# One 512 KB transfer for a cache page's keys and values, in one slot held until the value products

## The chip, the cores and the metric

The kernel runs on one core of a Trainium2 chip. The metric is the device time of one execution in microseconds (us). Before the change it was 1029.4 us, the median of 3 runs (1027.76 to 1031.65).

## What is computed

One layer of a decoder step for 544 tokens of 1024 channels: 512 tokens of a new prompt, and 32 sample tokens (8 sequences of 4 tokens), which continue sequences of 4096 past positions. All of it is in 32-bit floating point.

```python
glu_a, glu_b, q, k, v, g_conv, g_att = split(x @ w_in)            # 512,512,512,512,512,1024,1024 columns
conv_out = silu(layer_norm(depthwise_conv31(glu_a * sigmoid(glu_b)))) @ w_conv_proj
att_out  = stick_breaking_attention(q, [past_k, k], [past_v, v]) @ w_att_proj    # 8 heads of 64
x = layer_norm(ALPHA * x + (sigmoid(g_conv) * conv_out + sigmoid(g_att) * att_out) @ w_out)
gate, up = split(x @ w_ffn_up)                                    # 2 * 2816 columns
x = layer_norm(ALPHA * x + (silu(gate) * up) @ w_ffn_down + sigmoid(x @ w_ple_gate) * (p @ w_ple))
# for each query, positions s before it, from the last to the first:
#   weight(s) = exp(log_sigmoid(z_s) + sum over later t of log_sigmoid(-z_t)),  z = q . k / 8 + bias
```

The past keys and values of the 8 sample sequences lie in a pool of 320 pages of 128 positions; `page_table` names the 32 pages of each sequence. A page in the kernel's layout is 128 rows of 4 KB: in each row 2 KB belong to the keys (transposed: 4 pairs of heads by 128 positions) and the next 2 KB to the values of one position. The cache that is read has 8 x 32 pages of 512 KB, 134 MB.

## The kernel before

**One instruction order, made by a planner.** The kernel is written as Python generators ("streams"): the dense products (`main`), the weights' loader and splitter, the convolution, the prompt's attention, the loads of the cache (`prefetch`), the scores over the cache (`scores`), the rest of the cache attention (`decode`), and the sample tokens' way to the first norm (`sample_tail`). A class `Weave` runs them and emits their instructions in one order by estimated times: TensorE's clock `t`, and clocks for ScalarE, VectorE, GpSimd and the DMAs. A stream that yields a number, a time or a condition is resumed when the estimated clock is there; the first stream in order of priority that can go is taken, and the dense products come last. On the chip each engine takes its instructions in that order and waits on semaphores; the planner's times matter only for the order. `moved` adds a transfer to the DMA clock: a start 1.5 us ahead at the earliest, and its bytes divided by 0.357e6 per us; `load` counts the tile as there 1.5 us later.

**Dense products.** A weight unit is 128 x 1024 (512 KB), loaded on SyncE's queue (SP) and split in two parts, so that each product is three products (`g<-xh,wh` and the like in the profile). The sequence is: 20 column tiles for q, k, conv and v; 8 tiles for the attention gate (flags `("ga", c)`); 8 for the convolution's gate (flags `("gc", c)`); the attention's projection (its end sets the flag `"ga"`); the convolution's projection; `w_out` in two passes over halves of the prompt; the feed-forward's first 4 column tiles with the first 256 tokens, then the same with all others. This last pass needs the sample tokens' first norm, so it waits for the whole cache attention and `sample_tail`. After it come the rest of the feed-forward and the second norm.

**The cache attention.** It has 32 steps ("chunks"): 4 sequences by 2 pages each, 16 chunks from the last position to the first, and then the other 4 sequences. Of one chunk:

- `prefetch` loads in SP's queue: first the keys, then the values; a slot of 512 KB takes the keys (or values) of both pages of one sequence, by two transfers of 256 KB. The page's number is read into a register ahead of each keys' transfer (L536) and used again for the values. So there are 4 slots of keys and 4 of values for each chunk.
- `scores` (L552): 16 products of 32 queries with 256 positions into bank `z`, four sequences side by side in TensorE's columns (the trace shows each as two matmuls). Then its 4 slots are free: `cur["kv"] -= 4`. ScalarE follows with four operations on `zb` and `l`.
- `decode` (L605): VectorE's running sum over positions, which carries on from the chunk before, an exponential, two transposes, a copy, and then the value products `av`, 8 products with 512 columns (16 matmuls in the trace). Then the 4 slots of values are free.

**Room.** `slot` takes one of 39 slots of 512 KB, which dense tiles use too. `room_kv` lets `prefetch` go on only while the cache holds fewer slots than allowed at this place of the order:

```python
KVMAX = 17
KVROOM = (("ga", 17), (("gc", 0), 13), (("ga", 4), 15))
```

so 17 until the fifth gate tile of the attention, then 15, from the first gate tile of the convolution 13, and from the end of the attention's projection 17 again. `sample_tail` takes its 12 weight units under the same limit once all of the cache is loaded. `KMARGIN` = 1.0 us stands between a chunk's last key and its scores.

Of the kernel before, what the change touches and what calls it, by code (L numbers as in the profile page):

```python
# [20 lines left out]
NT = 544          # 512 prompt tokens, then 32 sample tokens  # L21
HT = 272
HA = 256          # the first half of the tokens in the passes that take them by halves
KW = 31
NPG = 32
POOL = 320
NA = 4            # column tiles of the feed-forward that start with half of the tokens
EMB = (1, 2)
FA = []           # their units of weights, and those of w_ple between them
# [8 lines left out]
# where a unit lies: the passes over the second half of the tokens take weights again  # L38
# [4 lines left out]
# columns of the vector table  # L43
# [6 lines left out]
class At:  # L50
    """A time to wait for."""
# [5 lines left out]
class Weave:  # L57
    """Emits the steps of several streams in one program order, by estimated times of the engines."""
# [9 lines left out]
    def op(self, clock, us, out, reads):  # L68
        """An instruction's estimated time: returns its end."""
        start = max([getattr(self, clock), self.t] + [self.ready.get(a.name, 0.0) for a in reads])  # L70
        setattr(self, clock, start + us)
        self.ready[out.name] = max(self.ready.get(out.name, 0.0), start + us + LAT)

    def take(self, tag, tile, bufs=1):
        """A new owner of a bank: it may be written when the one before has been read."""
# [5 lines left out]
    def bank(self, tag):  # L81
        """True when the bank's owner has been read."""
        return lambda: not self.owner.get(tag) or self.read.get(self.owner[tag][0], 1e9) <= self.t
# [44 lines left out]
class Engine:  # L128
    """An engine's instructions, with their estimated times."""
# [39 lines left out]
def step_kernel(ctx: ExitStack, tc: tile.TileContext, xT, pT, kv, state, pt, W, cv, cc, yT, kT, vT, cvo):  # L169
# [15 lines left out]
    def spare(n):  # L185
        """Waits until n of the short-lived tiles can be had."""
# [12 lines left out]
    def room():  # L199
        """Waits until the bank pair that comes next will have been read."""  # L200
# [13 lines left out]
    def moved(ap):  # L214
# [3 lines left out]
        wv.dma = max(wv.dma, wv.t + 1.5) + n / 0.357e6  # L218
# [36 lines left out]
    def tt(out, in0, in1, op):  # L255
        """An operation of two tensors in SBUF, on the vector engine or on GpSimd."""
# [27 lines left out]
    def sigmoid(out, in_, t, t2, then, more=None):  # L284
        """out = exp(-(max(-x, 0) + log(1 + exp(-|x|)))); t2 views t in the form of in_."""
# [42 lines left out]
    def held(u):  # L328
        """Where a unit's parts stay while both halves of the tokens need them."""
# [13 lines left out]
    def w_split(u, e):  # L343
        """Half a unit's parts."""
# [53 lines left out]
    def passes(p, cols, k, nk, w, x):  # L398
        """The three products of a tile's parts."""
# [30 lines left out]
    def norm(xs, sc, n, tag, buf, total, each, gain=None, pace=None):  # L430
        """xs: pairs of tiles; sc: 1024 over the channels; total: the tiles' sum; buf: pairs' room."""
# [86 lines left out]
    def room_kv():  # L518
        """True while the cache's blocks leave the room that the dense part comes to need."""
# [3 lines left out]
    def prefetch():  # L523
        for c in range(NCH):
            r, n = divmod(c, 16)
            reg = {}
            for part in range(2):
                for j in range(4):
                    yield room_kv
                    cur["kv"] += 1  # L530
                    t = slot("kv", (128, 2, 512))
                    for g in range(2):
                        yield lambda: wv.dma - wv.t < DMA_AHEAD
                        col = (4 * r + j) * NPG + 30 - 2 * n + g
                        if part == 0:
                            reg[col] = nc.sync.value_load(ptt[0:1, col:col + 1], min_val=0, max_val=POOL - 1)  # L536
                        load(nc.sync, t[:, g, :],
                             kv[bass.ds(reg[col], 1), :, part * 512:(part + 1) * 512].rearrange("o p c -> (o p) c"))
                    kv_t[c, part, j] = t
# [12 lines left out]
    def scores():  # L552
        for c in range(NCH):
            r = c // 16
            yield lambda: (c, 0, 3) in kv_t and c - n_scan[0] < 2
            ks_ = [kv_t.pop((c, 0, j)) for j in range(4)]
            yield on(*ks_)
# [3 lines left out]
            for m in range(4):  # L561
                for j in range(4):
                    mm(0.127, z[32 * j:32 * j + 32, :256].rearrange("p (g c) -> p g c", g=2),
                       qblk[:, 4 * r + j, m, :], ks_[j][:, :, m * 128:(m + 1) * 128], m == 0, m == 3)
            del ks_
            cur["kv"] -= 4
# [6 lines left out]
    def decode():  # L573
# [27 lines left out]
        for r in range(2):  # L601
# [3 lines left out]
            for n in range(16):  # L605
# [22 lines left out]
                yield lambda: (c, 1, 3) in kv_t  # L628
                kvs = [kv_t.pop((c, 1, j)) for j in range(4)]
                yield on(*kvs)  # L630
                for g in range(2):
                    for j in range(4):
                        mm(0.235, av[32 * j:32 * j + 32, :], at[:, g * 128 + 32 * j:g * 128 + 32 * j + 32],
                           kvs[j][:, g, :], n == 0 and g == 0, False)
                del kvs, zb, l, at, p
                cur["kv"] -= 4
# [20 lines left out]
    pa = {"live": 0, "next": 0}  # L657

    def pa_pair(idx, m, tiles):
        """Blocks of queries of both heads of a pair, side by side in the array."""  # L660
# [885 lines left out]
```

## Time and profile before

| | |
|---|---|
| runs, median (range) | 1029.4 us (1027.76 to 1031.65) |
| span of the profiled execution | 1028.2 us, clock 0.987 |
| TensorE matmul busy | 978.4 us (95%) |
| VectorE, ScalarE, GpSimd busy | 635.7, 484.7, 165.2 us |
| moved by DMA | 222.00 MB, mean 216 GB/s |
| cache transfers | 512 of 256 KB, first issue at 16.1 us, last at 542.6 us |
| first scores, last value products | 66.0 us, 556.9 us |
| second pass of the feed-forward's first tiles begins | 585.3 us |

The profiled execution took 1028.2 us from its first instruction to its last; no time around that span is listed for it, and the runs' median lies 1.2 us above it. PE is TensorE's matmuls, PEld its weight loads, DVE VectorE, ACT ScalarE, POOL GpSimd, SP SyncE and SPq SyncE's issuing of transfers. "Busy" of PE includes time in which a matmul's operands were late within a group.

### The profile page before, as it was taken

The numbers are of one execution on the slowest core, as the hardware profiler recorded it, in microseconds if no ns is written. First come the engines' busy times: TensorE is split into PE (matmuls) and PEld (weight loads), VectorE is DVE, ScalarE is ACT, GpSimd is POOL, SyncE is SP. The second block draws the span as 40 slices with busy tenths as digits, with TensorE's granted clock in tenths as the row PEclk, the third lists the DMA queues.
The fourth block names the chain that finished last, engine by engine and source line by source line (L and its number), as shares of the span: only waits on it lengthen the run. The fifth ranks groups of instructions, "written<-read, shape, count | busy, mean of one in ns | idle before, by whom it ended". The sixth has DMA issues, their size and how long they took to land.

```text
span 1028.2 us, 22484 instructions
## 1 busy us (share of the span) xinstructions
PE 978.4 (95%) x8242; PEld 856.4 (83%) x8242; DVE 635.7 (62%) x1005; ACT 484.7 (47%) x941; POOL 165.2 (16%) x156
## 2 busy tenths in 40 slices
PE   7988998999899999999999899999999999999994
PEld 6866576677677876788777899999999999999993
DVE  4798899999847457475796753433343345323376
ACT  4634666566786874344566553332333232212224
POOL 1320322313112002133332200000000012000021
PEclk9999999999999999999999999999999999999998
DMA  9959989999899999999999352232223222322302
GB/s 354 313 178 326 314 269 337 324 327 325 287 296 315 334 325 326 342 330 342 316 330 386 111 181 83 83 94 92 84 84 101 83 83 84 101 83 82 124 1 87
DMA packets 101375, 222.00 MB, mean 216 GB/s; under 512 B 11153, under 2 KB 14482, under 8 KB 101266
## 3 DMA queue, kind: packets, MB, share of 16 engines
q1 hardware_dynamic: 99394, 217.46, 62.3%
q10 hardware_dynamic: 1872, 3.11, 0.8%
q8 instruction: 65, 1.06, 0.4%
q14 instruction: 44, 0.36, 0.1%
HBM read 215.45 MB, written 5.07 MB: 214 GB/s over the span
## 4 chain that ended last, share of the span: by engine, by line
PE 70%; DVE 13%; DMA 8%; issue 3%; SPq 3%; ACT 2%; POOL 0%; ACTq 0%; DVEq 0%; POOLq 0%
PE g L231 58%; DMA kv<-in_kv 5%; PE z L231 5%; DVE c L139 4%; PE av L231 4%; DVE pb L139 2%; SPq L221 2%; SPq L536 1%; PE tp L236 1%; PE o L231 1%; DMA xr<-in_xT 1%; DVE dl L139 1%; DMA wq<-in_W 1%; DVE pa L139 1%; DVE wl L139 1%
## 5 line engine op out<-in xcount | busy, mean ns | idle before, releaser
L139 ACT ACTIVATE wh<-wr 128x512 fp32r<-128x512 f32 x236 | 146.8, 628 | 295.1 <-PE g L231 252.4
L139 DVE TENSOR_TENSOR wl<-wr,wh 128x512 fp32r<-128x512 f32 x193 | 134.0, 700 | 167.3 <-ACT wh L139 166.2
L231 PE MATMUL g<-x1h,wh 128*128 128x272 f32 (+2 forms) x832 | 183.7, 289 | 2.3 <-ACT x1h L139 1.6
L231 PE MATMUL g<-x1h,wl 128*128 128x272 f32 (+2 forms) x832 | 182.5, 288 | 0.0
L231 PE MATMUL g<-x1l,wh 128*128 128x272 f32 (+2 forms) x832 | 182.1, 288 | 0.0
L139 POOL TENSOR_TENSOR wl<-wr,wh 128x512 fp32r<-128x512 f32 x47 | 68.5, 1460 | 535.7 <-ACT wh L139 494.5
L231 PEld LDWEIGHTS g<-x1h,wh 128*128 128x128 f32 x832 | 134.8, 188 | 4.6 <-ACT x1h L139 1.7
L231 PEld LDWEIGHTS g<-x1l,wh 128*128 128x128 f32 x832 | 134.8, 189 | 0.0
L231 PEld LDWEIGHTS g<-x1h,wl 128*128 128x128 f32 x832 | 134.0, 189 | 0.0
L231 PE MATMUL g<-xh,wh 128*128 128x272 f32 (+1 forms) x512 | 128.3, 322 | 5.8 <-ACT wh L139 5.8
L231 PE MATMUL g<-h,wh 128*128 128x272 f32 x704 | 122.2, 290 | 0.0
L231 PE MATMUL g<-xh,wl 128*128 128x272 f32 (+1 forms) x512 | 120.1, 306 | 0.2 <-POOL wl L139 0.2
L231 PE MATMUL g<-xl,wh 128*128 128x272 f32 (+1 forms) x512 | 120.2, 306 | 0.0
L139 DVE SCALAR_TENSOR_TENSOR c<-u,cvt,c 128x512 f32<-128x512 f32 x120 | 112.3, 936 | 3.3
L231 PEld LDWEIGHTS g<-xh,wh 128*128 128x128 f32 x512 | 83.8, 193 | 27.2 <-issue 17.5
L231 PEld LDWEIGHTS g<-h,wh 128*128 128x128 f32 x704 | 103.1, 189 | 0.3
L231 PEld LDWEIGHTS g<-xh,wl 128*128 128x128 f32 x512 | 83.7, 192 | 3.9 <-POOL wl L139 0.8
L231 PEld LDWEIGHTS g<-xl,wh 128*128 128x128 f32 x512 | 84.1, 192 | 2.7 <-DVE xl L139 0.5
L231 PE MATMUL g<-h,wl 128*128 128x272 f32 x352 | 80.1, 289 | 0.0
L231 PE MATMUL z<-kv,qblk 128*32 128x256 f32 x1024 | 67.0, 382 | 3.7 <-DMA kv<-in_kv 3.7
L231 PE MATMUL av<-kv,dp 128*32 128x512 f32 x512 | 64.0, 612 | 0.0
L139 ACT ACTIVATE pa<-pa 128x384 f32<-128x384 f32 (+1 forms) x96 | 52.5, 555 | 17.0 <-DVE pa L139 15.4
(222 smaller groups left out, 1398.0 us busy)
## 6 DMA issues: line engine op xcount, KB each, us to landing
kv<-in_kv SPq DMA_DIRECT2D x512, 256.0 KB, 5.3
wr<-in_W SPq DMA_DIRECT2D x120, 512.0 KB, 3.5
wq<-in_W SPq DMA_DIRECT2D x15, 512.0 KB, 6.7
wa<-in_W SPq DMA_DIRECT2D x12, 512.0 KB, 9.9
xr<-in_xT SPq DMA_DIRECT2D x8, 272.0 KB, 5.7
out_yT<-pw SPq DMA_DIRECT2D x7, 272.0 KB, 2.3
out_kT<-qk ACTq DMA_DIRECT2D x4, 272.0 KB, 5.5
out_vT<-vt ACTq DMA_DIRECT2D x4, 272.0 KB, 4.4
```

The lines of the kernel that those rows point to most:

```text
L139: fn(**kw)
L221: eng.dma_start(out=out, in_=in_)
L231: T.matmul(out, lhsT=lhsT, rhs=rhs, start=start, stop=stop)
L236: T.transpose(out, in_, ident)
L536: reg[col] = nc.sync.value_load(ptt[0:1, col:col + 1], min_val=0, max_val=POOL - 1)
```

## The change

Each page comes with its keys and values in one transfer of 512 KB into a slot of its own, 8 slots to a chunk; the slot is given back after the value products, and no longer half of them after the scores. The page's number is read once for each transfer, as before 256 times in all. The score products take one page at a time: 128 columns in place of 256 and twice as many. `KVMAX` and `KVROOM` stay as they are. The planner's rate for all DMAs goes from 0.357e6 to 0.385e6 bytes per us, and its time for a score product from 0.127 to 0.06 us. (Comments and docstrings are gone as well, which changes no instruction.)

```diff
@@ moved
-        wv.dma = max(wv.dma, wv.t + 1.5) + n / 0.357e6
+        wv.dma = max(wv.dma, wv.t + 1.5) + n / 0.385e6
@@ prefetch
             r, n = divmod(c, 16)
-            reg = {}
-            for part in range(2):
-                for j in range(4):
+            for j in range(4):
+                for g in range(2):
                     yield room_kv
                     cur["kv"] += 1
-                    t = slot("kv", (128, 2, 512))
-                    for g in range(2):
-                        yield lambda: wv.dma - wv.t < DMA_AHEAD
-                        col = (4 * r + j) * NPG + 30 - 2 * n + g
-                        if part == 0:
-                            reg[col] = nc.sync.value_load(ptt[0:1, col:col + 1], min_val=0, max_val=POOL - 1)
-                        load(nc.sync, t[:, g, :],
-                             kv[bass.ds(reg[col], 1), :, part * 512:(part + 1) * 512].rearrange("o p c -> (o p) c"))
-                    kv_t[c, part, j] = t
+                    t = slot("kv", (128, 1024))
+                    yield lambda: wv.dma - wv.t < DMA_AHEAD
+                    col = (4 * r + j) * NPG + 30 - 2 * n + g
+                    reg = nc.sync.value_load(ptt[0:1, col:col + 1], min_val=0, max_val=POOL - 1)
+                    load(nc.sync, t, kv[bass.ds(reg, 1)].rearrange("o p c -> (o p) c"))
+                    kv_t[c, j, g] = t
@@ scores
-            yield lambda: (c, 0, 3) in kv_t and c - n_scan[0] < 2
-            ks_ = [kv_t.pop((c, 0, j)) for j in range(4)]
-            yield on(*ks_)
+            yield lambda: (c, 3, 1) in kv_t and c - n_scan[0] < 2
+            ks_ = [[kv_t[c, j, g] for g in range(2)] for j in range(4)]
+            yield on(*[t for x in ks_ for t in x])
...
             for m in range(4):
-                for j in range(4):
-                    mm(0.127, z[32 * j:32 * j + 32, :256].rearrange("p (g c) -> p g c", g=2),
-                       qblk[:, 4 * r + j, m, :], ks_[j][:, :, m * 128:(m + 1) * 128], m == 0, m == 3)
+                for g in range(2):
+                    for j in range(4):
+                        mm(0.06, z[32 * j:32 * j + 32, g * 128:(g + 1) * 128], qblk[:, 4 * r + j, m, :],
+                           ks_[j][g][:, m * 128:(m + 1) * 128], m == 0 and g == 0, m == 3 and g == 1)
             del ks_
-            cur["kv"] -= 4
@@ decode
-                yield lambda: (c, 1, 3) in kv_t
-                kvs = [kv_t.pop((c, 1, j)) for j in range(4)]
-                yield on(*kvs)
+                kvs = [[kv_t.pop((c, j, g)) for g in range(2)] for j in range(4)]
...
-                           kvs[j][:, g, :], n == 0 and g == 0, False)
+                           kvs[j][g][:, 512:1024], n == 0 and g == 0, False)
                 del kvs, zb, l, at, p
-                cur["kv"] -= 4
+                cur["kv"] -= 8
```

## The prediction

> **What bounds the kernel now.** I read the page first (span, the chain that ended last, the groups of the two cache products), then windows, the chain in order of time, and SP's own queue.
>
> ```profile
> span 1028.2 us, 22484 instructions
> PE 978.4 (95%) x8242; PEld 856.4 (83%) x8242; DVE 635.7 (62%) x1005; ACT 484.7 (47%) x941; POOL 165.2 (16%) x156
> PE 70%; DVE 13%; DMA 8%; issue 3%; SPq 3%; ACT 2%; POOL 0%; ACTq 0%; DVEq 0%; POOLq 0%
> L231 PE MATMUL z<-kv,qblk 128*32 128x256 f32 x1024 | 67.0, 382 | 3.7 <-DMA kv<-in_kv 3.7
> ```
>
> PE is busy 978.4 of 1028.2 us, so no faster transfer can win more than the 49.8 us in which it isn't. The cache's scores waited for DMA only 3.7 us before a group, and their busy time holds a little more of it.
>
> What sets the pace of the cache is seen in the chain (start, length, what) around an early chunk and two later ones, and in SP's queue:
>
> ```profile
> 66.09 1.86 PE z L231 x32
> ...
> 337.32 0.34 SPq L221
> 338.50 0.34 SPq L221
> 344.63 3.24 DMA kv<-in_kv
> 348.00 1.67 PE z L231 x25
> 360.52 3.74 DMA kv<-in_kv
> ```
>
> ```profile
> 440.63 5.39 SPq L221 DMA_DIRECT2D kv<-in_kv  x9
> ```
>
> Keys with a page number to read are issued 1.18 us apart (337.32 to 338.50), values, whose number is known, 5.39 / 9 = 0.60 us apart. A chunk costs SP 8 x 1.18 + 8 x 0.60 = 14.2 us, with two weight units at 0.6 us 15.4 us; the last keys of two following chunks stand 15.9 us apart (344.63 and 360.52). So SP's issuing, not the DMA engines, paces the cache; PE fills the time with dense products, which are emitted between the cache's steps.
>
> **The change, part by part.**
>
> *Fewer issues, larger transfers.* A chunk then has 8 issues with a number, 8 x 1.18 = 9.4 us, and 1.2 us for weights: 10.6 us of SP, 4.8 less. What the DMA engines can do is seen where weights of 512 KB are loaded alone, and what they do beside the cache in the third row (last columns: DMA share, GB/s):
>
> ```profile
> 10.00:20.00 10.00, 10.00 (x41) 7.81 (x39) 3.92 (x7) 3.37 (x6) 0.00 (x0) 1.00 1.03 406
> 550.00:560.00 10.00, 8.29 (x66) 5.65 (x65) 9.17 (x18) 7.21 (x18) 4.55 (x7) 1.00 1.03 408
> 100.00:500.00 400.00, 385.88 (x3273) 295.80 (x3274) 297.44 (x465) 247.57 (x496) 94.87 (x88) 0.98 0.94 320
> ```
>
> At 407 GB/s a page takes 0.524 MB / 407 = 1.29 us, a chunk 10.3 us and with two weight units 12.9 us, against 15.9 now. [...]
>
> What is won on PE are its waits at the scores: 3.7 us before them, and inside them the busy 67.0 us less 32 undisturbed chunks at 1.86 us (the row of 66.09), 59.5, are 7.5. I take **-10 us**; the bounds are 0 (other waits end in the same place) and -49.8.
>
> *Score products by page.* 64 matmuls of 128 columns in place of 32 of 256. The trace has the same shape, with 32 queries against 128 columns in four column groups, in the tail: 64 in 1.95 and 1.89 us, where 32 of 256 took 1.86.
>
> ```profile
> 479.20 1.93 PE L231 MATMUL z<-kv,qblk 128*32 128x256 f32 x32
> 487.95 1.92 PE L231 MATMUL av<-kv,dp 128*32 128x512 f32 x16
> ```
>
> ```profile
> 562.69 1.95 PE z L231 x64
> 564.64 0.95 PE g L231 x6
> 565.81 1.43 PE g L231 x12
> 567.24 1.89 PE z L231 x64
> 569.12 1.26 PE g L231 x9
> 572.27 0.91 PE g L231 x6
> 585.28 3.45 PE g L231 x24
> ```
>
> Bounds -1 and +1 us over 32 chunks; I take **+1**.
>
> *Slots held to the value products.* This is the part that I think decides. The order is the planner's, so its clock must be followed: now a chunk takes it 8 x 0.524 / 0.357 = 11.75 us and 1.47 for a weight unit. How much room a stage has follows from the flags, whose places are these:
>
> ```profile
> L139 ACT ACTIVATE ga<-ga x24: 640/657/664, 236.3 to 327.0; 128x544 f32<-128x544 f32 x24
> L139 ACT ACTIVATE gc<-gc x24: 639/657/667, 330.9 to 398.5; 128x544 f32<-128x544 f32 x24
> L139 DVE TENSOR_TENSOR ga<-g,ga x8: 677/691/693, 399.1 to 424.9; 128x512 f32<-128x512 f32 x8
> ```
>
> The fifth of eight gate columns ends at about 285 us (between 236.3 and 327.0): 17 slots until there, 15 to about 337, 13 to 425, then 17 again. Now 12 slots hold a chunk in its chain and the next one's keys and values, and the keys go early: the loads never stop. After the change 13 slots hold the chunk in its chain (8) and only 5 pages of the next; its other 3 wait for the value products. From these to the next scores the planner then counts 1.5 + 3 x 1.36 + 1.5 + 1.0 (`KMARGIN`) = 8.1 us (1.36 = 0.524 / 0.385). From scores to the end of the value products a chunk takes at best 487.95 + 1.92 - 479.20 = 10.7 us, and 17.2 in this row pair, where the chunk before stood ahead:
>
> ```profile
> 334.41 1.90 PE z L231 x26
> 349.68 1.93 PE av L231 x14
> ```
>
> I take 12.5 here, nearer the first because nothing stands ahead any more: a period of 20.6 us, bounds 18.8 and 25.3. Now:
>
> ```profile
> kv<-in_kv SPq DMA_DIRECT2D x88, 256.0 KB, 5.5
> wr<-in_W SPq DMA_DIRECT2D x10, 512.0 KB, 6.4
> wq<-in_W SPq DMA_DIRECT2D x1, 512.0 KB, 6.9
> ```
>
> From 337 to 425 us 88 transfers are 5.5 chunks, with 11 weight units, 2 a chunk: 11.75 + 2 x 1.47 = 14.7 us of planner time. PE needs 3.9 us of a period for the chunk (1.93 + 1.92); the rest is dense. Dense work ends the stage: 5.5 x 10.8 = 59 us of it at 16.7 a period are 3.6 chunks. **The cache falls 1.9 chunks behind.** With 15 slots 1 page is missing: 1.5 + 1.36 + 1.5 + 1.0 = 5.4, and with 14 for the chain (the convolution's work is on DVE there) a period of 19.4: (337 - 285) / 15.9 = 3.3 chunks by the same reckoning become 2.3, **1.0 behind**. With 17 slots two chunks are in turn: two periods are 7 pages and a weight unit, 1.5 + 8 x 1.36 + 1.5 + 1.0 = 14.9, and the chain's 14, so 14.4 a chunk against 13.2 to 14.7 now. Over 13 chunks that is at most 1.1; the start adds some:
>
> ```profile
> 77.54 1.85 PE av L231 x16
> 79.39 1.73 PE z L231 x32
> 103.73 3.67 PE av L231 x16
> ```
>
> The third chunk's scores stand at 79.39 right behind the first value products, because the first scores gave slots back; now they must wait for 7 pages, to about 79.4 + 7 x 1.29 + 5.5 (the landing of the cache's row above) = 94, and their value products (103.73) move little. For both I take **1.5 chunks**. Together 4.4 (bounds 1.5 and 7).
>
> *The end.* Of the scores these stand behind 425 us:
>
> ```profile
> 425.00:559.00 134.00, 16.48 (x256) 1.00 0.97 338
> ```
>
> 256 / 32 = 8 chunks are left there now, then 12.4. What covers them is dense work before the feed-forward's second pass:
>
> ```profile
> 559.00:585.00 26.00, 15.59 (x114) 1.00 0.55 199
> 425.00:559.00 134.00, 97.87 (x749) 1.00 0.97 338
> ```
>
> 15.6 + 97.9 = 113.5 us of `g`. A period there with 17 slots is two in 1.5 + 9.5 + 2.7 + 2.5 + 11.5, so 13.9, and with 2 weight units the planner's DMAs give 13.6; less 3.9 it is 10 of dense work, on the chip 10.9 (the row of 565.81 has 119 ns a matmul of 256 columns, the planner counts 109). 113.5 / 10.9 = 10.4 chunks are covered, **2.0 are not**. An uncovered chunk lasts (7 x 1.29 + 5.5 + 10.7) / 2 = 12.6 us and PE works 3.9 of it: 8.7 x 2.0 = **+17 us**. Then the tail from the last value products to 585.28 has no dense work left beside it: its 15.6 us of `g` have run earlier, while the tail shortens only by those that stand in its chain (0.95 + 1.43 + 1.26 + 0.91 = 4.6) and perhaps by 1.7 at its start: **+9 us** (bounds 0, where work is left, and 15.6). What else waits: `sample_tail` takes its 12 weight units under the same 17 slots, and the last 3 can be issued only after the last value products; 3 x 1.29 + 5.5 = 9.4 us lie beside the 8 us from there to the second pair of products (567.24), so 0 (at most +3). On SP's queue weights stand behind a page that waits for a slot; the loader lets four units run ahead, at least 4 x 24 x 119 ns = 11 us of products, so I take 0; where that cover goes, PE waits for weights.
>
> After 585 us nothing is changed. Sum: 1028.2 - 10 + 1 + 17 + 9 = 1045.2, and as the runs' median stands 1.2 us above the profiled execution **1046 us**, slower. A lag of 3.4 would give 1.0 uncovered, +9 and +9, 1038; one of 7, the bound, 4.6 uncovered, +40 and +9, 1069: the case's own range is 1036 to 1068.
>
> **The rivals.**
>
> *The cache keeps its place (faster).* The same mechanism from the other side: at most 10.4 chunks may be left at 425 us, a lag of 2.4, and all of them are covered; then only the waits count: 1028.2 - 10 + 1 and the 1.2, **1020**. For it: the late stage runs faster, 13.9 for 14.7, and the chain in the 13-slot stage could be the 10.7 of the best row. Against: that still gives 18.8 against 14.7.
>
> *Nothing to be told.* At a lag of 3, 0.6 uncovered chunks, +5, and half of the tail's 9 stand against -10 and +1: about **1030**. Less than 0.5%, about 5 us, can't be told from no change here.
>
> *Weights are starved too.* A page that waits for a slot stops SP, and the weights behind it. With some 6 chunks at 13 or 15 slots and 4 us each (8.1 less the 4.1 that 3 pages take), +24: **1070**. For it: SP's order is fixed; against: the 11 us above.
>
> *A matmul has a fixed cost.* If each of the 2,048 score matmuls took the 58 ns of one with 256 columns (1.86 / 32), 59.5 us came on PE: **1105**. The rows of 562.69 and 567.24 us speak against it, 30 ns each. [...]
>
> **How the numbers follow.** Forecast 0.52; starved weights 0.12; nothing to be told 0.16; keeps its place 0.17; fixed cost 0.03. Slower by over 0.5% is 0.52 + 0.12 + 0.03 = 0.67, the same 0.16, faster 0.17. The range reaches from 1020 (half of the faster case lies below) to 1068 (half of the starved case and the fixed cost above): a little under 2 in 10 outside.
>
> **What would show it.** Scores and value products would alternate with about 19 to 22 us between scores from 337 us on, with DMA's share falling well below 0.94 there; more than 8 chunks would stand behind the end of the attention's projection; after the last of `w_out`'s products PE would idle between cache products, and the tail would show little `g`. The step on issues is right if SP's pages come 1.2 us apart and the DMA rate reaches 400 GB/s in bursts. The forecast is wrong if the last value products come before about 560 us with `g` still beside the tail: then the lag was smaller, or was made up faster than 13.9 us a chunk.

## The result, and the profile after

The changed kernel took 1075.9 us (median of 4 runs, 1075.5 to 1077.1) against 1028.6 (4 runs of the kernel before beside it): the ratio is 1.046, 95% interval 1.043 to 1.050, so 47 us slower. The direction of the forecast holds, and the hold of the slots makes most of the loss, as it said; its size (17 us) was too small, and the time lies above the range. Of all the executions behind the times below one, of light365, took 2675.55 us; it isn't in that kernel's ratio.

The page of the changed kernel: span, engines, the 40 slices of TensorE, of its granted clock and of the DMA engines, the chain, the two cache products (busy us, mean ns | idle before them) and the cache's transfers (KB each, median us to landing):

```profile
span 1074.5 us, 23603 instructions
PE 989.5 (92%) x9266; PEld 880.5 (82%) x9266; DVE 635.6 (59%) x1008; ACT 486.4 (45%) x938; POOL 162.9 (15%) x156
PE   7979898988999999999976669999999999999994
PEclk9999999999999999999986889999999999999997
DMA  9919587682985789996899914222222222322402
PE 70%; DVE 21%; issue 3%; ACT 3%; DMA 2%; SPq 1%; POOL 0%; DVEq 0%; ACTq 0%
L231 PE MATMUL z<-kv,qblk 128*32 128x128 f32 x2048 | 66.5, 281 | 1.6 <-ACT pa L139 1.5
kv<-in_kv SPq DMA_DIRECT2D x256, 512.0 KB, 6.3
```

VectorE's share of the chain grows from 13% to 21%: its running sums and the convolution in front of them now lie on it. Two places stand out. In slices 3 to 19 the DMA engines often stand at 5 to 8 tenths: the cache's loads stop and start. In slices 21 to 24 (about 540 to 640 us) TensorE falls to 6 or 7 tenths and its clock to 6 to 8, and in the first three of them the DMA engines are full. Busy TensorE before and after 550 us, of the changed kernel (first column after the window: its length, then TensorE busy; the last three columns are clock, DMA share, GB/s):

```profile
0.00:550.00 550.00, 513.89 (x5248) 427.29 (x5248) 424.51 (x682) 332.63 (x666) 135.07 (x133) 0.99 0.77 284
550.00:631.40 81.40, 46.77 (x647) 25.61 (x645) 17.44 (x48) 17.14 (x44) 2.77 (x6) 0.77 0.83 329
631.40:1074.50 443.10, 428.84 (x3374) 427.63 (x3374) 193.64 (x279) 136.61 (x231) 25.04 (x17) 0.98 0.28 88
```

and the same two stretches of the kernel before, parted at the start of the feed-forward's second pass (585.3 us there, 631.4 here):

```profile
0.00:585.30 585.30, 550.75 (x4869) 430.49 (x4869) 439.42 (x722) 345.40 (x705) 140.21 (x139) 0.99 0.91 312
585.30:1028.20 442.90, 427.61 (x3374) 425.93 (x3374) 196.26 (x285) 139.27 (x238) 25.03 (x17) 0.99 0.28 89
```

From the second pass on both take 443 us, so the whole loss is made before it: 631.4 - 585.3 = 46.1 us. Up to there TensorE idled 585.3 - 550.8 = 34.6 us before and 36.1 + 34.6 = 70.7 after: 36.2 us of the loss. The other 9.9 are longer busy time (560.7 us for 550.8): twice as many score products of half the columns, and the same work besides.

Dense products alone (`g`, TensorE's busy time in three stretches of the changed kernel) say what is missing after 550 us:

```profile
395.00:548.00 153.00, 111.23 (x841) 1.00 0.89 336
548.00:611.00 63.00, 2.18 (x18) 0.76 1.02 408
611.00:632.00 21.00, 0.64 (x2) 0.83 0.23 92
```

All dense work that may run ahead of the second pass is done at 550 us. Then the cache runs alone at 408 GB/s to 611, and the sample tokens' tail alone to 631. The chain there, in order of time (start, length, what):

```profile
555.01 3.64 PE av L231 x16
558.65 2.81 PE z L231 x64
...
566.21 3.64 PE av L231 x16
569.84 2.15 PE z L231 x64
...
594.44 6.40 DMA kv<-in_kv
...
631.36 8.69 PE g L231 x50
```

Scores stand 11.2 us apart (558.65 to 569.84): a chunk's way through the slots and DMA engines, with nothing beside it. The value products take up to 3.64 us for 16 matmuls (granted clock in it 0.50) and the scores 2.81 for 64 (0.73), where the same groups take 1.9 from 395 to 548 us, at a clock of 1.00.

How far the cache had fallen behind is read from the count of `av` matmuls in the stages of the dense work: to the fifth gate tile, to the convolution's gate, to the end of the attention's projection. 16 are a chunk (8 in the third row close the first 16 chunks). The kernel before:

```profile
0.00:289.00 289.00, 28.62 (x224) 0.97 0.89 304
289.00:330.00 41.00, 6.63 (x56) 1.00 0.92 312
330.00:425.00 95.00, 14.18 (x112) 1.00 0.96 327
```

and after:

```profile
0.00:281.00 281.00, 23.24 (x176) 0.98 0.70 262
281.00:314.00 33.00, 3.85 (x32) 1.00 0.86 304
314.00:395.00 81.00, 6.63 (x56) 1.00 0.72 252
```

(The 8 closing matmuls are in the second row of the kernel before.) At the same places of the dense work 14, 17 and 24 chunks were through before, and 11, 13 and 16 after: a lag of 3, 4 and 8 chunks. The dense work reached the last place 30 us sooner, at 395 in place of 425, because 8 chunks' products weren't mixed in (8 x 3.9 = 31 us of TensorE); they came back later, and five chunks then have no cover.

### The profile page after: what moved, and what is told of

Same layout as the page of the kernel before. It is cut to its first block, busy times and chain, and to the rows that moved or that the text cites. A ratio compares the mean times of both kernels' runs of the same rounds, so it can differ in the third digit from the quotient of the medians.

```text
span 1074.5 us, 23603 instructions
## 1 busy us (share of the span) xinstructions
PE 989.5 (92%) x9266; PEld 880.5 (82%) x9266; DVE 635.6 (59%) x1008; ACT 486.4 (45%) x938; POOL 162.9 (15%) x156
## 4 chain that ended last, share of the span: by engine, by line
PE 70%; DVE 21%; issue 3%; ACT 3%; DMA 2%; SPq 1%; POOL 0%; DVEq 0%; ACTq 0%
PE g L231 58%; DVE c L139 8%; PE z L231 5%; PE av L231 5%; DVE pb L139 2%; DVE dl L139 2%; DVE wl L139 1%; DVE rr L139 1%; DMA kv<-in_kv 1%; PE tp L236 1%; DVE pa L139 1%; DVE dz L139 1%; DVE dp L139 1%; PE o L231 1%; DVE ln L139 1%
## 5 line engine op out<-in xcount | busy, mean ns | idle before, releaser
L139 ACT ACTIVATE wh<-wr 128x512 fp32r<-128x512 f32 x239 | 149.1, 628 | 305.4 <-PE g L231 256.7
L139 DVE TENSOR_TENSOR wl<-wr,wh 128x512 fp32r<-128x512 f32 x196 | 138.6, 713 | 179.2 <-ACT wh L139 176.1
L139 POOL TENSOR_TENSOR wl<-wr,wh 128x512 fp32r<-128x512 f32 x44 | 64.4, 1466 | 526.4 <-ACT wh L139 514.9
L139 DVE SCALAR_TENSOR_TENSOR c<-u,cvt,c 128x512 f32<-128x512 f32 x120 | 108.5, 904 | 3.3
L231 PE MATMUL av<-kv,dp 128*32 128x512 f32 x512 | 71.9, 685 | 2.8 <-ACT dp L139 2.8
L231 PEld LDWEIGHTS z<-kv,qblk 128*32 128x32 f32 x2048 | 58.1, 113 | 14.2 <-issue 4.7
L231 PE MATMUL z<-kv,qblk 128*32 128x128 f32 x2048 | 66.5, 281 | 1.6 <-ACT pa L139 1.5
```

The source lines that it names most:

```text
L139: fn(**kw)
L231: T.matmul(out, lhsT=lhsT, rhs=rhs, start=start, stop=stop)
```

## The experiments

Each kernel ran with the kernel before on the same chip (1028.6 to 1030.6 us); ratios are to that. "Order" below is the count of running sums that the planner puts ahead of the end of the attention's projection (24 of 32 before, 17 after), and "uncovered" the chunks whose running sum it puts behind the last dense product (0 before, 6 after): both are read from the program, not timed.

### The hold alone, and degrees of it

**hold_alone.** The kernel before with one edit: the four key slots are given back with the values, and no longer after the scores. Transfers, score products and planner's rate are as before.

```diff
-            ks_ = [kv_t.pop((c, 0, j)) for j in range(4)]
+            ks_ = [kv_t[c, 0, j] for j in range(4)]      # popped with the values
...
-            cur["kv"] -= 4          # after the scores
...
-                cur["kv"] -= 4      # after the value products
+                cur["kv"] -= 8
```

> The kernel before (two transfers of 256 KB, scores of 256 columns, planner rate 0.357), with one change: the slots of a chunk's keys are given back only after its value products. If holding the slots is what costs (theory: the cache falls behind in the order and its last chunks stand without dense work), this loses most of it: 1050 to 1065 us, with two or three chunks behind the last dense products where before had none; less than the change, because scores still wait for the keys alone. If the larger transfers, the smaller products or the planner's rate are the reason (rival), 1026 to 1032.

1067.3 us, ratio 1.037 (1.034 to 1.040), 2 us above the range. The hold by itself makes 38 of the 47 us. The order has 20 running sums at the projection's end and 2 uncovered chunks. Windows of the stretch without dense work, all engines:

```profile
565.00:622.00 57.00, 28.95 (x341) 14.79 (x339) 11.96 (x36) 9.78 (x27) 2.04 (x5) 0.86 0.74 270
```

TensorE idles 28 us in it, at a clock of 0.86.

**release_at_scores.** The changed kernel with all 8 slots given back right after the scores. The value products read the resident queries in place of the page's values, so their results are not those of the reference.

```diff
-            ks_ = [[kv_t[c, j, g] for g in range(2)] for j in range(4)]
+            ks_ = [[kv_t.pop((c, j, g)) for g in range(2)] for j in range(4)]
...
             del ks_
+            cur["kv"] -= 8
...
-                           kvs[j][g][:, 512:1024], n == 0 and g == 0, False)
+                           qblk.rearrange("p a m c -> p (a m c)")[:, 0:512], n == 0 and g == 0, False)
```

> The changed kernel, with the slots given back after the scores; the value products read a resident tile of the same shape in place of the pages' values (so the attention's values are left out, every product and transfer is there). Theory of the hold: no chunk stands behind the dense work any more and the loss is gone, 1015 to 1030 us. Rival (transfers, product form or planner rate): it stays above 1055 us.

1037.0 us, ratio 1.007 (1.004 to 1.009). 39 of the 47 us come back, and the cache is early (order 27; last value products end at 517 us). It is above the range that was expected by 7 us; release357 below says why.

**release_exp.** The same, value products on the resident queries too, but the slots are given back later, ahead of the chunk's transposes: between the two.

```diff
                 tp = bank("tp")
+                for j in range(4):
+                    for g in range(2):
+                        kv_t.pop((c, j, g))
+                cur["kv"] -= 8
                 for g in range(2):
                     tr(tp[:, g * 128:(g + 1) * 128], zb[:, g * 128:(g + 1) * 128])
```

> The changed kernel, with a chunk's slots given back ahead of its two transposes, that is after the running sum and the exponential; the value products read the resident queries in place of the page's values. It holds a slot longer than to the scores (1037 us) and some 5 to 8 us shorter than to the value products (1076). Theory 1, the time that a slot is held sets how far the cache falls behind, and the uncovered chunks set the time: in the planner's order 20 running sums stand before the end of the attention's projection (17 with the full hold, 27 with the release at the scores) and 1 chunk is left without dense work, so 10 us for it and 5 to 9 for the tail above the release at the scores: 1045 to 1058 us. Theory 2, what was regained at the release at the scores came from the other operand of the value products (no wait for a page's values) and not from the slots: 1034 to 1041 us.

1051.6 us, ratio 1.021 (1.015 to 1.027), inside the range of theory 1; order 20, 1 uncovered. With the same operand as in the run before, a longer hold costs 15 us: the time follows the hold, not the operand. Its stretch without dense work:

```profile
573.00:606.00 33.00, 19.06 (x314) 11.33 (x307) 9.93 (x29) 5.82 (x15) 0.00 (x0) 0.80 0.57 224
```

Over the kernels with a hold:

| kernel | without dense work, us | second pass begins | time | profiled execution less that start |
|---|---|---|---|---|
| before | none over 3.5 behind 425 us | 585 | 1028.6 | 444 |
| release_exp | 33 | 606 | 1051.6 | 445 |
| hold_alone | 56 | 622 | 1067.3 | 445 |
| room17 (below) | 53 | 625 | 1072.2 | 447 |
| kmargin0 (below) | 64 | 631 | 1074.4 | 446 |
| after | 81 | 631 | 1075.9 | 445 |
| rate357 (below) | 103 | 643 | 1088.4 | 446 |

The last column hardly moves, so what a kernel loses it loses before the second pass, which waits for the whole cache.

### What sets the loop's pace

**room17.** The changed kernel with 17 slots all the way: `KVROOM` with 17 in place of 15 and 13.

```diff
-KVROOM = (("ga", 17), (("gc", 0), 13), (("ga", 4), 15))
+KVROOM = (("ga", 17), (("gc", 0), 17), (("ga", 4), 17))
```

> The changed kernel with 17 slots allowed for the cache throughout, in place of 15 and then 13 in the gates' stage. The prediction put 2.9 of its 4.4 chunks of lag into those stages; with them lifted, about 2 to 3 chunks less lag at some 6 to 9 us each: 1050 to 1062 us. If the 17-slot stage before makes nearly all of the lag, 1068 to 1077. If dense tiles run short of slots instead, slower than 1076.

1072.2 us, ratio 1.041 (1.039 to 1.044): 4 us of the 47, in the second of the three ranges. 18 chunks are through at the projection's end in place of 16, and the last scores come 10 us sooner. So the tighter stages, on which the forecast laid 2.9 of its 4.4 chunks, are a small part; when they begin the cache is already late.

**rate357.** The changed kernel with the planner's old DMA rate (0.385e6 back to 0.357e6).

```diff
-        wv.dma = max(wv.dma, wv.t + 1.5) + n / 0.385e6
+        wv.dma = max(wv.dma, wv.t + 1.5) + n / 0.357e6
```

> The changed kernel with the planner's rate for transfers put back to 0.357. Theory of the hold: the rate is not the cause, and slower planned loads make the lag a little longer, 1074 to 1088 us. Rival (the faster rate made a bad order): 1030 to 1050 us.

1088.4 us, ratio 1.055 (1.051 to 1.059): 103 us without dense work, where

```profile
540.00:643.00 103.00, 59.92 (x808) 32.76 (x806) 18.54 (x52) 21.09 (x52) 1.85 (x5) 0.78 0.85 331
```

With the hold, loads lie inside the loop, and what the planner counts for them (8 x 0.1 us more a chunk) puts the cache further back in the order. The bolder rate, part of the change, saves 12 us of what the hold costs. So the parts don't simply add up: at the same rate of 0.357e6 this kernel is 21 us above hold_alone (1088.4 to 1067.3). Both hold 8 slots to the value products, but here the scores wait for all 8 pages, values included, and there for the 4 slots of keys; whether that, the product form or the transfers make the 21 us isn't separated.

**kmargin0.** The changed kernel with `KMARGIN` 0 in place of 1.0 us, a plain shortening of the planner's loop.

```diff
-KMARGIN = 1.0
+KMARGIN = 0.0
```

> The changed kernel without the planner's 1.0 us between a chunk's last page and its scores. If the loop from value products through loads to scores sets the cache's pace (theory 2), each loop is 1 us shorter in the order, one chunk and a half less lag over some 25 loops at 6 to 10 us each: 1058 to 1070 us. If the pace is set elsewhere, 1072 to 1080.

1074.4 us, ratio 1.045 (1.041 to 1.048): no change within the intervals, though the order has only 3 uncovered chunks in place of 6. The dense work lasts longer (to 567 us), but the tail ends at 631 as in the changed kernel (the profiled execution, 1077.4 us, is 3 us above this kernel's median):

```profile
567.00:631.00 64.00, 35.48 (x480) 20.75 (x480) 13.73 (x39) 11.25 (x28) 0.76 (x4) 0.76 0.71 273
```

The loop does become shorter where the slots set it: in the 17-slot stage the scores stand 18.8 us apart in place of 20.0, and the thirteenth chunk's come at 281 us in place of 294. The lead is gone at the end: the last chunk's scores come at 599 us, and at 600 in the changed kernel. Between 549 and 568 us SyncE issues only 5 pages, with 4 weight units in between, so at 568 us it is only 3 pages ahead of the changed kernel (19 left to issue, and 22). That an earlier order in the first stage would carry through to the end was expected wrongly.

**taps5_before, taps5_after.** Both kernels with 5 of the convolution's 31 taps left, which takes 83 us of work from VectorE (635.7 to 552.3 in the kernel before); the convolution's result is then another.

```diff
-                for k in range(KW):
+                for k in range(5):
                     w = cvt
```

> The kernel before with 5 of the 31 taps of the prompt's convolution (26 taps left out): about 94 us less work on VectorE in the stage with 17 slots. It is the base for the next kernel. VectorE is busy over 90% in that stage, PE too, so a small gain: 1012 to 1028 us.

> The changed kernel with 5 of 31 taps. If the chain from scores to value products is long in the 17-slot stage because it stands behind the convolution on VectorE (theory 1: the 14 us of the prediction would then be right without it), the cache keeps up there and the distance to the kernel above shrinks to 10 to 28 us. If the pace is the planner's order itself (theory 2: pages can be asked for only after the value products, and the planner places these late for other reasons, as the prompt's attention in the same banks), 38 to 52 us stay.

1023.5 us (0.994, 0.991 to 0.997) and 1059.1 us (1.030, 1.026 to 1.034). The distance falls from 47 to 36 us, between the two ranges: with VectorE relieved a chunk's way from scores to value products is 17 us in place of 21 in the first stage (means of chunks 2 to 11), and the scores follow 17.5 us apart in place of 20. But the dense work becomes faster as well (the fifth gate tile at 262 us), and again 11 chunks are through at that place. Taking VectorE's load away takes a quarter of the loss away.

### SyncE's issuing, and the planner's rate

**split_alone.** The kernel before with the score products by 128 columns.

```diff
-                for j in range(4):
-                    mm(0.127, z[32 * j:32 * j + 32, :256].rearrange("p (g c) -> p g c", g=2),
-                       qblk[:, 4 * r + j, m, :], ks_[j][:, :, m * 128:(m + 1) * 128], m == 0, m == 3)
+                for g in range(2):
+                    for j in range(4):
+                        mm(0.06, z[32 * j:32 * j + 32, g * 128:(g + 1) * 128], qblk[:, 4 * r + j, m, :],
+                           ks_[j][:, g, m * 128:(m + 1) * 128], m == 0 and g == 0, m == 3 and g == 1)
```

> The kernel before with the score products by pages alone: 128 columns, twice as many, planner time 0.06. By the rows of the tail (64 in 1.89 us against 32 in 1.86) it costs 1 us: 1024 to 1034 us. If a matmul has a fixed cost of the size of the present one, 1085 to 1090.

1034.1 us, ratio 1.0044 (1.0022 to 1.0067): 4.5 us, at the range's edge, more than the +1 of the rows; its order also differs, and which of the two makes the rest stays open.

**fixed_pages.** The kernel before with page numbers written into the program in place of the lookup (so it reads other pages than the table's).

```diff
-                            reg[col] = nc.sync.value_load(ptt[0:1, col:col + 1], min_val=0, max_val=POOL - 1)
+                            reg[col] = col
...
-                             kv[bass.ds(reg[col], 1), :, part * 512:(part + 1) * 512].rearrange("o p c -> (o p) c"))
+                             kv[reg[col]:reg[col] + 1, :, part * 512:(part + 1) * 512].rearrange("o p c -> (o p) c"))
```

> The kernel before with the pages at fixed places, so that no page number is read (the page table's lookup is left out; the transfers and the order are the same). SP then needs 0.6 us for each transfer and no longer paces the cache. The prediction put 10 us of waits at the scores down to that pace: 1017 to 1021 us if it was right. If other waits on PE end in the same place, 1024 to 1030.

1018.9 us, ratio 0.987 (0.984 to 0.991). Taken away in the old order, SyncE's work on page numbers is worth 11 us: the forecast's -10 was there to be had.

**light_lookup.** The kernel before, still reading the page table, but without the check of each number against a lowest and a highest value.

```diff
-nc.sync.value_load(ptt[0:1, col:col + 1], min_val=0, max_val=POOL - 1)
+nc.sync.value_load(ptt[0:1, col:col + 1])
```

> The kernel before, with the page number read without the bound check's instructions. SP's issue with a number should fall from 1.18 to about 1.0 us, a chunk from 15.4 to 14.0. If SP's pace costs PE anything, 1020 to 1027 us, about half of what fixed pages win; if not, 1026 to 1031.

1021.1 us, ratio 0.992 (0.989 to 0.995): the best kernel of the study that computes the whole layer, 8 us faster than the kernel before and 55 faster than the changed one. It has 512 instructions less, two for each page. The scores' wait is gone and their busy time is near the 59.5 us of undisturbed chunks:

```profile
span 1019.1 us, 21972 instructions
L231 PE MATMUL z<-kv,qblk 128*32 128x256 f32 x1024 | 62.7, 381 | 0.1
```

**after_light.** The same edit in the changed kernel.

```diff
-                    reg = nc.sync.value_load(ptt[0:1, col:col + 1], min_val=0, max_val=POOL - 1)
+                    reg = nc.sync.value_load(ptt[0:1, col:col + 1])
```

> The changed kernel, its page numbers read without the check against a lowest and a highest value (a page's issue on SyncE becomes shorter, the order stays the same). Theory 1, in the changed order SyncE doesn't set the pace, slots do: 1073 to 1079 us, no change. Theory 2, SyncE's issues still pace it, as they did the kernel before, which the same edit made 8 us faster: 1064 to 1070 us.

1076.5 us, ratio 1.044 (1.038 to 1.050): nothing. In the changed kernel SyncE's issues don't set the pace; that the slots do is what hold_alone and the two releases show.

**before385.** The kernel before with the planner's rate alone at 0.385e6.

```diff
-        wv.dma = max(wv.dma, wv.t + 1.5) + n / 0.357e6
+        wv.dma = max(wv.dma, wv.t + 1.5) + n / 0.385e6
```

> The kernel before with the planner's rate at 0.385 alone. The order then puts scores earlier among the dense work than SP can feed them. If the rate alone were good, 1018 to 1024 us; if SP's pace makes PE wait for keys, 1032 to 1050.

1071.9 us, ratio 1.039 (1.035 to 1.042), beyond the second range. The order now puts the scores earlier than their keys come, and TensorE stands ahead of the scores for 26 us, and 15 more inside them (busy 82.2 for 67.0). Whether SyncE or the DMA engines (0.91 to 0.97 busy between 66 and 550 us) hold the keys back, this run doesn't tell:

```profile
L231 PE MATMUL z<-kv,qblk 128*32 128x256 f32 x1024 | 82.2, 406 | 26.2 <-DMA kv<-in_kv 26.1
```

**light365 and light350.** The light lookup with the planner's rate at 0.365e6 and 0.350e6, 2% to either side.

```diff
-        wv.dma = max(wv.dma, wv.t + 1.5) + n / 0.357e6
+        wv.dma = max(wv.dma, wv.t + 1.5) + n / 0.365e6      # light350: 0.350e6
```

> The kernel before with the page number read without the bound check's instructions and the planner's rate at 0.365. SP then issues a chunk in 14 us, so the order may be a little bolder: 1014 to 1022 us if SP keeps up; 1025 to 1040 if SP is late for it, as at 0.385.

> The kernel before, its page numbers read without the check against a lowest and a highest value (1021 us), and the planner's DMA rate at 0.350 in place of 0.357. If SyncE is still a little late for the order, as 1027 us at 0.365 suggests, a calmer order gains: 1014 to 1020 us. If at 0.357 the order and SyncE already agree, the cache only comes later: 1020 to 1027 us.

1027.0 us (0.997, 0.995 to 0.999) and 1037.1 us (1.008, 1.005 to 1.011). The first lies in its second range, but not for the reason given there: TensorE waits only 0.5 us for keys ahead of the scores. The second lies outside both ranges. Of it the windows show that TensorE was less busy in both of these stretches (the rows of light350, then of light_lookup, which has the same lookup at 0.357):

```profile
122.00:245.00 123.00, 114.73 (x997) 86.91 (x996) 115.70 (x181) 77.95 (x162) 36.54 (x35) 0.97 0.85 290
245.00:560.00 315.00, 302.94 (x2600) 239.79 (x2599) 213.87 (x349) 188.39 (x378) 68.73 (x68) 0.98 0.91 320
```

```profile
122.00:245.00 123.00, 117.42 (x1022) 86.95 (x1019) 116.07 (x185) 77.17 (x158) 34.79 (x33) 0.99 0.93 320
245.00:560.00 315.00, 307.20 (x2773) 244.89 (x2771) 218.98 (x356) 196.72 (x397) 69.16 (x65) 0.99 0.93 329
```

That is 7 us more idle time. In it TensorE waits 4.2 us ahead of two scores for the cache, where light_lookup doesn't, and 3.3 us for the prompt's `v` in place of 0.8; and the second pass begins 14 us later (590.6 to 576.2). Why 2% of the planner's rate to either side does this stays open; the time doesn't follow the rate smoothly.

**release357.** release_at_scores with the planner's rate back at 0.357e6.

```diff
-        wv.dma = max(wv.dma, wv.t + 1.5) + n / 0.385e6
+        wv.dma = max(wv.dma, wv.t + 1.5) + n / 0.357e6
```

> The changed kernel with the slots given back at the scores (value products on the resident queries) and the planner's DMA rate at its old 0.357. It asks why that kernel stayed 8 us above the one before (1037 against 1029) although its cache is early. Theory 1, the bolder rate places the steps of the chain earlier than ScalarE and VectorE can serve, and TensorE waits at the transposes: with the old rate 1018 to 1028 us. Theory 2, the products by page or the 512 KB transfers themselves cost it: 1033 to 1040 us.

1029.3 us, ratio 0.999 (0.997 to 1.002), just above theory 1's range: the 8 us that were missing at the release at the scores come from the bolder rate. Up to the second pass TensorE's waits in front of transposes fall from 18.6 us to 10.9, as theory 1 had it, but mostly at the prompt's own (`pa`: 8.5 to 2.9); the cache's chain (`dz`, `dp`) makes TensorE wait 5.5 us in one and 4.5 in the other. So that it is the softmax chain that is late isn't shown. And the change without its hold and without its planner's rate, that is, 512 KB transfers and products by page, is worth nothing either way. What eats the relief of SyncE is not shown; the 4.5 us of split_alone may be part of it.

## Why the forecast was right in kind and wrong in size

**What would show it** came, most of it as listed: DMA's share at 0.72 in the 13-slot stage, 16 chunks left behind the projection's end, TensorE idle between cache products after the last dense product, and 0.64 us of `g` beside the tail. Only the scores stand further apart in that stage, 24 us in place of 19 to 22.

**The issue of pages: right, and worth nothing here.** SyncE's issues in the changed kernel are 1.1 to 1.2 us apart where they come in a row, 8 a chunk. The rate reaches 408 GB/s over 63 us (548 to 611), as in the two rows of 10 us by which the sum went (406 and 408).

**-10 us from waits at the scores: failed.** The waits in front of the scores went (3.7 to 1.6 us), as the step said, but the sum took it that nothing takes their place: a bound of 0 for "other waits end in the same place" was named, and -10 taken. Up to 550 us TensorE idled 36.1 us, more than the kernel before in its whole 585 (34.6). Its longest waits from 66 us to the end of the dense work (us in total, times, longest), after and then before:

```profile
PE tp L236 <- DVE v L139: 7.4, 3, 3.3
PE tp L236 <- ACT pa L139: 6.0, 3, 3.0
PE tp L236 <- DVE vs L139: 3.9, 2, 3.1
```

```profile
PE tp L236 <- ACT pa L139: 7.2, 4, 2.4
PE z L231 <- DMA kv<-in_kv: 3.7, 7, 0.9
PE z L231 <- ACT dz L139: 2.3, 1, 2.3
```

Waits of the prompt's own transposes (`v`, 7.4 us in place of 1.3, and `vs`, 3.9) stand where the waits for keys stood; why they are longer in the new order isn't shown. The relief was real in the old order (fixed_pages, light_lookup) and is none in the new one (after_light).

**+1 for products by page.** 1.88 us for 64 (at 230.86 and 241.68 in the chain) against 1.86 for 32: right as a duration; split_alone measured 4.5 us as an edit.

**The lag: the step that failed.** 4.4 chunks were forecast and 8 measured at the projection's end, one above the bound of 7. Stage by stage:

- *17 slots.* 1.5 forecast, 3 measured. The start came as expected: the third chunk's scores were put at 94 us and stand there,

```profile
94.01 1.95 PE L231 MATMUL z<-kv,qblk 128*32 128x128 f32 x64
```

and the thirteenth's at

```profile
294.24 1.75 PE z L231 x64
```

So 10 chunks took 200.2 us, 20.0 each, where (14.9 + 14) / 2 = 14.4 were forecast. Of the two terms the chain from scores to the end of the value products was taken as 14 and measures 21.1 (mean of chunks 2 to 11, counted from 0), and the loads after it as 14.9 and measure 18.5: (21.1 + 18.5) / 2 = 19.8. The 14 was a choice for which the forecast shows no row of this stage; apart from the first chunk's 13.4 us, chains of about that length stand in the kernel before only from 393 us on (13.1 to 15.5 us up to 457). In the stage itself the kernel before shows 23.2 us (mean of the same chunks), and the forecast had quoted one of them: scores at 79.39, value products at 103.73 + 3.67, 28 us. While keys went early that length cost nothing, so it didn't show in the times; a hold turns it into the pace. That pages now wait for value products is seen in SyncE's waits up to 640 us, after and then before:

```profile
SPq L221 <- PE av L231: 38.1, 20, 14.3
```

```profile
SPq L221 <- PE av L231: 1.9, 6, 0.4
```

The planner's own clock has a part of it: in the changed kernel it lays the scores of chunks 2 to 12 down 17.1 us apart (17.6 for the chain, 16.6 for the loads), so about half of the miss (2.7 of 5.6 us a chunk) stands in the order before any chip runs it. A part of the rest is in SyncE's queue, where at one place weights stand ahead of pages:

```profile
235.94 26.79 SPq L221 DMA_DIRECT2D wr<-in_W  x3
263.56 6.47 SPq L221 DMA_DIRECT2D kv<-in_kv  x6
```

No page is issued from 229.8 to 263.6 us. The value products that free the next slots end at 255.1, and the third weight unit, which waits 12.8 us for its buffer, holds the pages back 8.5 us longer.
- *15 slots.* A lag of 1.0 forecast, 1 measured.
- *13 slots.* 1.9 forecast, 4 measured. The places of the gates in the changed kernel,

```profile
L139 ACT ACTIVATE ga<-ga x24: 639/656/674, 237.8 to 313.4; 128x544 f32<-128x544 f32 x24
L139 DVE TENSOR_TENSOR ga<-g,ga x8: 678/688/692, 369.2 to 394.4; 128x512 f32<-128x512 f32 x8
```

put it at 314 to 395 us. Scores there stand 24 us apart (315, 339, 363, 388 us) where 20.6 were forecast, and 3 chunks come through: the chain was taken as 12.5 and measures 15.7, the loads behind it as 8.1 and measure 8.7 (means of those three steps). The kernel before brought 7 chunks in this stage, not the 5.5 by which the forecast counted.

**Uncovered chunks.** Covered after the projection's end: 10.4 forecast, 10 through at 550 us and the eleventh begun, in 153 us. Left over: 2.0 forecast, 5 with their scores behind 548 us. These stand 9.6 to 12.5 us apart, 10.8 on average, not 12.6 (at the 408 GB/s of this stretch 8 pages take 10.3), so a chunk costs less than forecast, but two and a half times as many pay it.

**The tail: right.** `g` beside it fell to 0.64 us, and it took the forecast +9 or a little less: TensorE idled 10.0 us in the third row below, and 3.4 in the first, which is the kernel before; the second is the stretch of uncovered chunks.

```profile
559.00:585.30 26.30, 22.95 (x331) 20.86 (x323) 14.27 (x31) 10.61 (x26) 5.32 (x5) 1.00 0.55 201
```

```profile
548.00:611.00 63.00, 38.36 (x454) 19.50 (x453) 11.36 (x27) 16.82 (x40) 2.77 (x6) 0.76 1.02 408
611.00:632.00 21.00, 11.01 (x216) 8.68 (x211) 6.68 (x24) 2.58 (x9) 0.00 (x0) 0.83 0.23 92
```

**The clock, not in the sum.** The work of the stretch without dense products ran at 0.76 and 0.83 of full clock. The groups of 548 to 611 us (busy us, mean ns):

```profile
L231 PE MATMUL av<-kv,dp 128*32 128x512 f32 x96 | 19.8, 967 | 2.8 <-ACT dp L139 2.8
L231 PE MATMUL z<-kv,qblk 128*32 128x128 f32 x320 | 13.4, 319 | 0.1
```

96 / 16 = 6 groups of value products in 19.8 us are 3.3 each, and 320 / 64 = 5 of scores in 13.4 are 2.7, where 1.9 is usual: 8.4 + 4.0 us, which more than answers for the 9.9 us by which TensorE's busy time grew. From the end of one score group (558.65 + 2.81) to the next value products (566.21) only two transposes stand in 4.8 us, the longest wait among them 3.6, and 16 matmuls then take 3.64 us, about twice 1.9. The clock granted in those 3.64 us is 0.50, and 0.63 where 16 take 2.94 (from 576.49); in the kernel before 16 take 1.92 at 1.00 (from 487.95). So the longer groups go with a lower clock; what lowers it is not shown.

The 46.1 us in the forecast's terms: idle time before the dense work ends +4.9 (36.1 us, where the kernel before has 34.6 less the tail's 3.4) in place of -10; in uncovered chunks 24.6 (63.0 - 38.4) in place of 17; the tail 10.0 - 3.4 = 6.6 in place of 9; the clock 9.9, which the sum didn't have (the +1 for products by page is in it). So of the 29 us that the sum fell short, 14.9 are the -10 that became +4.9, 8.9 the clock, 7.6 the uncovered chunks, and the tail gives 2.4 back. Of the rivals, weights starved too came nearest in time (1070) but isn't the cause: between 66 and 550 us the changed kernel's list of TensorE's waits has no weight part in it. What the queue shows is rather the reverse, pages behind weights. A fixed cost per matmul is excluded by split_alone (1034.1 us, where it was to give 1085 or more), and the faster case by the lag.

## What to carry to other kernels

Before a buffer is held longer, measure the length of the work that it is then held through in the very stage where the hold will bite: a latency that costs nothing while loads run ahead becomes the loop's period when the slots are the limit (23 us stood in the trace of that stage; 14 was taken). Count the lag in units of that loop at each place of the dense work and ask when the cover ends, for here uncovered work paid twice, in idle time (24.6 us) and in a slower TensorE clock (0.76 in that stretch, some 9 us). And test the cheap part alone: some 8 of the 11 us that SyncE's page lookups cost were a bounds check, which can be left out without any hold where the page numbers are sure to be valid.

## What the runs showed of the hardware

- One core's transfers held 408 GB/s over 63 us (548 to 611 us of the changed kernel), at 512 KB each.
- TensorE's mean granted clock was 0.76 from 548 to 611 us of the changed kernel, where it was 61% busy (38.4 of 63 us), and groups of 16 matmuls of 512 columns took up to 3.64 us there, at a clock of 0.50, in place of 1.9 at 1.00. In the stretches without dense work of hold_alone and release_exp the clock was 0.86 (28.95 of 57 us busy) and 0.80 (19.06 of 33).
- An indexed transfer's issue on SyncE came 1.17 us behind the last with the number's bounds checked and 0.58 where the number was already read (medians of the kernel before), and 0.86 without the check (light_lookup from 299.85 us: 8 in a row in 6.34 us, the last 0.33 of them its own issue). Leaving the 256 checks out was worth 8 us to the kernel before, and nothing to the changed one.
